# A grouped-query entry with two weight splits moved, and a last norm whose gain ScalarE multiplies ahead of time

## The chip, the cores and the metric

The kernel runs on one core of one Trainium2 chip. The metric is the time of one execution on the device, in microseconds (us). Five engines work side by side, each through its own instructions in order: TensorE (PE, matrix products), VectorE (DVE, element by element), ScalarE (ACT, functions of one tensor), GpSimd (POOL) and SyncE (SP, which here only issues transfers). Transfers between the chip's main memory and the on-chip buffers run on sixteen DMA engines; SP, ACT and POOL each have a queue from which they issue them.

## What is computed

One step of a small backbone with two layers, for 512 latent tokens and 128 prompt tokens with 1024 features each. Layer 0 mixes tokens by latent attention and neighbourhood attention, layer 1 by grouped-query attention (8 query heads, 2 key/value heads of 128 features, with 128 cached positions). Each mixer is followed by a gated feed-forward block, and the whole ends with a root-mean-square norm. Two pieces of the reference matter here: the entry of layer 1 and the last norm.

```
def odd_project(h, w_in, q_norm, k_norm):
    p = h @ w_in
    q, k, v = jnp.split(p, [...], axis=-1)
    q = rms_norm(q.reshape(b, L, GQA_HEADS, GQA_HEAD_DIM), q_norm)
    k = rms_norm(k.reshape(b, L, GQA_KV_HEADS, GQA_HEAD_DIM), k_norm)
    ...

def rms_norm(x, g):
    y = xf * lax.rsqrt(jnp.mean(xf * xf, axis=-1, keepdims=True) + RMS_EPS)
    return (y * g).astype(x.dtype)

y_prompt = rms_norm(xp, norm_final)
y_sample = rms_norm(xs, norm_final)
```

## The kernel before

**Layout.** Features lie on the 128 partitions and tokens along the free dimension. The 1024 features are eight tiles, `x[0]` to `x[7]`, of 128 x 640 (512 latent and 128 prompt tokens). A tile is worked on in two halves of 320 tokens (`HALF`, index c = 0 or 1).

**Split products.** Every float32 product is made from three products of rounded parts. An operand is split into a high part (a rounded copy, written by ACT) and a low part (the difference, written by DVE). `unit` (line 175) loads one 128 x 1024 weight tile and splits it: one ACT instruction (line 184), one DVE instruction (line 185). Its argument `behind` takes one instruction, or a pair (one for ACT, one for DVE), behind which the two are to be issued on their engines. The split weights share three places (tag "w", `bufs=3`), and the raw weights three others (tag "raw").

**What sets the order.** The program is written in one order, but a planner orders each engine's instructions: it goes through the program with estimated costs and puts an instruction that it thinks ready ahead of an earlier one that it thinks is not. Memory is handed out in the same pass. Three things bind it: data dependencies, `after(inst, fn)`, which makes what `fn` issues follow `inst` on the engine of `inst`, and `run`/`sequence`, which do the same for the pieces of PE's work, so that PE follows the order written out by hand (`GQA_FIRST`, line 2028, for head 0).

**The grouped-query entry (lines 1800 to 2040).** PE makes in turns the first half of the keys of group 0 (`keys(0, 0, ...)`, weights `wgk0`), the first half of head 0's queries (`wgq0`), and the values. The values of the 640 new tokens are five products of 128 tokens x 256 (`gvalues`); `gvo[0]` to `gvo[4]` share three banks of PSUM, the accumulator memory, two by two. Each runs over eight feature tiles: the first four use the weights `wgv0`, the last four `wgv1` (line 2011). A sixth value tile comes from the cache (`gcvf`). A loop (line 2015) splits the six into `gvh` and `gvl`; index 4 is the cached tile and index 5 is `gvo[4]`. It keeps the last pair of instructions in the list `valued`. Then head 0's last query products are made, the PSUM banks of keys and values are given back, and new ones are opened for the scores (line 2021, `open_y(s=2)`), so the first scores can't be written before all readers of the value banks are through.

Keys are normalised and rotated on DVE (`knorm`, `rope`), as queries are (`gqr`, `gqh`, `gql`). `weigh` (line 1954) turns a block's scores into exponentials: DVE multiplies the negative maximum by the query's factor `rq`, ACT makes the exponential. Head 0's sequence holds the keys of group 1 (`k0` to `k7`, weights `wgk1`, split at line 1884) and, at its end, head 1's queries (`q0` to `q7`, weights `wgq1`, line 1899).

**The end (lines 1640 to 1730 and 2068 to 2075).** The second half of the last feed-forward product is made in four passes p over pairs of output tiles, each with seven products (`S2, A11, S3, A12, A22, S1, S4`). For p = 3 the tiles are n = 6 and n + 1 = 7. `evac` adds a product to `x` (`residual`, line 319) and adds the square of the result to the norm's sum (`Norm.add`: ACT squares, DVE adds). `nrm.rstd(c)` sums over partitions with one PE product and makes the factor `nrm.rs` by a logarithm and an exponential on ACT. `final` (line 2068) then multiplies each half tile by the gain column and the factor in one DVE instruction (line 2073) and stores it (line 2074), even tiles from ACT's queue and odd ones from SP's. The tile `x[0]` is called `lead` in the profile and the others `xr`. Tile 0 of the first half is scaled before the last residual, tiles 1 to 7 after the last square is added, and then the second half follows.

Of the kernel before, what the change touches and what calls it, by code (L numbers as in the profile page):

```python
# [50 lines left out]
def body(ctx, tc, xT, vecs, crow, wm0, wm0g, wm1, wA, wNV, wNA, wMK, wMV, wOA, wGQ, wGK, wGV, wOC,  # L51
# [267 lines left out]
    def residual(xo, xi, ps, ml, g, n, i):  # L319

        o = HALF[i][0]
        for c0, c1, c in HCOND[i]:
            V.scalar_tensor_tensor(xo[:, c0:c1], ps[:, c0 - o:c1 - o], ml[:, g + n, c:c + 1], xi[:, c0:c1],
                                   ALU.mult, ALU.add)

# [859 lines left out]
    def ffn_open(l):  # L1185
# [13 lines left out]
        return ph, fk, dr, hd, fs, fp, w, pre  # L1199

    def ffn(l, x, pend, hm, nxt, side, opened):
        ph, fk, dr, hd, fs, fp, w0, _ = opened
# [431 lines left out]
        if paired:  # L1634
# [54 lines left out]
            for p in range(4):  # L1689
# [3 lines left out]
                for k, (c, which, to) in enumerate(PLAN):  # L1693
                    j = p * len(PLAN) + k
                    weights(j + LEAD)
                    seventh(j, b[to], which, c in ("S2", "A11", "S1", "S4"))
                    ps = b[to][:, :HT]
                    if c == "S2":
                        S.activation(o["p6"], ps, AF.Copy)
# [7 lines left out]
                    elif c == "A22":  # L1707
                        V.tensor_tensor(o["p1"], ps, o["p1"], ALU.add)
                        evac(n + 1, 0, o["p1"])
                        if p == 3:  # L1710
                            nrm.rstd(0)
                    elif c == "S1":
                        V.tensor_tensor(o["u3"], ps, o["u3"], ALU.add)
                        V.tensor_tensor(o["p6"], ps, o["p6"], ALU.add)
                        if p == 3:
                            residual(x[n], x[n], o["p6"], mods[l], G2, n, 1)
                            evac(n + 1, 1, o["u3"])
                            ended = after(nrm.last, lambda: nxt(x, nrm, 0, range(0, 1)))
                        else:
                            evac(n + 1, 1, o["u3"])  # L1720
                    elif p == 3:
                        after(ended, lambda: evac(n, 1, b["d"]))
                        after(nrm.last, lambda: nxt(x, nrm, 0, range(1, KT)))
                    else:
                        V.tensor_tensor(o["x"], ps, o["p6"], ALU.add)
                        evac(n, 1, o["x"])
# [151 lines left out]
    def keys(v, c, ks):  # L1878
# [4 lines left out]
        if v not in wk:  # L1883
            wk[v] = unit(wGK[v], 1024, f"wgk{v}")
        for k in ks:
# [9 lines left out]

    gqs, rope0, valued = {}, [], []

    def gqa_q(h):
        get = lazy(lambda: unit(wGQ[h], 1024, f"wgq{h}", behind=valued[0] if h == 1 else None))
        qh = gp.tile([P, T], F32R, tag="gqh", bufs=2, name=f"gqh{h}")  # L1900
# [31 lines left out]
    def gqa_scores(h, pts):  # L1932
# [3 lines left out]
        def piece(j):  # L1936
# [17 lines left out]
            def weigh():  # L1954
                V.tensor_tensor(nb, nm, rq[:, j:j + 1], ALU.mult)  # L1955
                S.activation(dst, src, AF.Exp, bias=nb, scale=rq[:, j:j + 1], accum_out=ll[:, j:j + 1])  # L1956
                softmax_tail(pt, ll[:, j:j + 1], f"gr{h}_{j}", n)
                pts.append(pt)
# [50 lines left out]
    for v in range(2):  # L2009
        ksplit(v, 512, 640, ckf[:, P * v:P * v + P])  # L2010
    gvalues(range(5), range(4, KT))
    gvh = [gp.tile([P, 256], F32R, name=f"gvh{i}") for i in range(6)]
    gvl = [gp.tile([P, 256], F32R, name=f"gvl{i}") for i in range(6)]
    srcs = gvo[:4] + [cvf, gvo[4]]
    for i in (0, 1, 2, 3, 5, 4):
        valued[:] = [(S.activation(gvh[i], srcs[i], AF.Copy), V.tensor_tensor(gvl[i], srcs[i], f(gvh[i]), ALU.subtract))]
# [51 lines left out]
    def final(x, nrm, c, ks):  # L2068
        c0, c1 = HALF[c]
        if 0 in ks and c == 1:  # L2070
            nrm.rstd(c)
        for k in ks:
            last = V.scalar_tensor_tensor(x[k][:, c0:c1], x[k][:, c0:c1], vcol(V_NFIN + k), nrm.rs[:, c0:c1], ALU.mult, ALU.mult)
            (nc.sync if k % 2 else nc.scalar).dma_start(yT[:, k, c0:c1], x[k][:, c0:c1])
        return last
# [160 lines left out]
```

## Time and profile before

| What | Value |
|---|---|
| Median of 3 runs | 1488.22 us (1488.15 to 1488.6) |
| Profiled execution, its own time | 1486.84 us |
| Its span | 1485.1 us |
| Granted TensorE clock, mean | 0.997 |
| PE busy | 1440.8 us, 97% of the span |
| DVE busy | 1210.7 us, 82% |
| ACT busy | 763.1 us, 51% |
| Moved by DMA | 228.61 MB, 154 GB/s on average |

The profile is one execution, recorded instruction by instruction. Its times count from the start of the span. A row of a timeline has the start, the duration, the engine, the line, the operation, the tiles (out<-in, with their sizes) and how many were merged; the brackets at its end tell how long the engine sat idle before it and which instruction released it. PEld is PE's loading of weights, which overlaps the products. SPq and ACTq are issues of transfers, not the transfers. A row of windows has, for one stretch, the busy time of PE, PEld, DVE, ACT and POOL, then the granted clock, the busy share of the sixteen DMA engines and the rate in GB/s.

### The profile page before, as it was taken

How to read it: one execution, taken by the hardware profiler on the slowest of the kernel's cores; microseconds unless marked ns; L12 is line 12 of the kernel's file. 1: busy time of each engine (PE TensorE's matmuls, PEld its weight loads, DVE VectorE, ACT ScalarE, POOL GpSimd, SP SyncE). 2: the span in 40 equal slices, each digit the busy share in tenths (PEclk: the TensorE clock that was granted, in tenths of full speed). 3: DMA queues.
4: the chain of work that ended last, by engine and by line, in shares of the span. 5: the costliest groups of instructions: out<-in, count | busy, mean ns of one | idle time of the engine just before them, and what ended most of it. 6: DMA issues, size and time to landing. Idle time of an engine off the chain costs nothing.

```text
span 1485.1 us, 25709 instructions
## 1 busy us (share of the span) xinstructions
PE 1440.8 (97%) x9785; PEld 1390.6 (94%) x9785; DVE 1210.7 (82%) x2278; ACT 763.1 (51%) x1509; POOL 209.9 (14%) x298
## 2 busy tenths in 40 slices
PE   5999989999999999999999999999999999999996
PEld 3988878889999999999999999989999999999996
DVE  5786798975999999977998878775899999954496
ACT  5445687863755444441123666663755555532242
POOL 0325544432000000000002322222000000000000
PEclk9999999999999999999999999999999999999998
DMA  9644511016055555569763301004055556668522
GB/s 370 220 146 141 177 49 33 29 33 209 29 195 176 191 186 183 172 226 340 266 214 125 105 29 45 29 32 133 31 188 175 188 189 208 214 222 304 195 86 72
DMA packets 79900, 228.61 MB, mean 154 GB/s; under 512 B 8864, under 2 KB 14272, under 8 KB 79392
## 3 DMA queue, kind: packets, MB, share of 16 engines
q1 hardware_dynamic: 76544, 219.40, 43.2%
q0 software_dynamic: 1600, 5.14, 0.9%
q10 hardware_dynamic: 1632, 2.43, 0.5%
q8 instruction: 77, 1.26, 0.3%
q14 instruction: 47, 0.39, 0.1%
HBM read 192.23 MB, written 34.69 MB: 153 GB/s over the span
## 4 chain that ended last, share of the span: by engine, by line
PE 84%; DVE 8%; ACT 5%; issue 2%; DMA 1%; SPq 0%; DVEq 0%; POOL 0%; ACTq 0%
PE fg L63 21%; PE fd L63 9%; PE fo L63 8%; PE fu L63 6%; PE gq L63 3%; PE nk L63 2%; PE fo_2b L63 1%; PE fo_0b L63 1%; PE gs L63 1%; PE nq L63 1%; PE fo_2a L63 1%; PE fo_0a L63 1%; PE go L63 1%; PE mod L63 1%; PE fo_4b L63 1%
## 5 line engine op out<-in xcount | busy, mean ns | idle before, releaser
L1774 DVE SCALAR_TENSOR_TENSOR junk<-wm,cb 128x1024 bf16<-128x1024 f32 x62 | 75.7, 1221 | 4.7 <-DMA wm<-in_wm 4.2
L1226 ACT ACTIVATE sg<-g 128x320 f32<-128x320 f32 x34 | 16.0, 472 | 114.8 <-DVE g L1226 114.8
L63 PE MATMUL gq<-h10h,wgq 128*128 128x320 f32 x256 | 66.7, 318 | 0.0
L255 POOL TENSOR_SCALAR h10h<-h10t,gs,mods 128x320 fp32r<-128x320 f32 x4 | 3.5, 887 | 429.5 <-DVE h10t L249 427.8
L1226 DVE SCALAR_TENSOR_TENSOR junk<-wm,cb 128x1024 bf16<-128x1024 f32 x50 | 61.0, 1221 | 0.8
L1226 DVE TENSOR_TENSOR wY<-s,wY 128x1024 fp32r<-128x1024 f32 x40 | 48.8, 1220 | 1.1 <-ACT wY L1226 1.1
L1226 DVE TENSOR_TENSOR wZ<-s,wZ 128x1024 fp32r<-128x1024 f32 x40 | 48.8, 1220 | 0.0
L63 PEld LDWEIGHTS gq<-h10h,wgq 128*128 128x128 f32 x256 | 45.0, 189 | 0.9 <-PE gtp L67 0.2
L1226 ACT ACTIVATE wZ<-s 128x1024 fp32r<-128x1024 f32 x40 | 42.4, 1060 | 0.2
L1226 ACT ACTIVATE wY<-s 128x1024 fp32r<-128x1024 f32 x40 | 42.0, 1049 | 0.0
L1956 ACT ACTIVATE gp<-gs,gb,rq 128x640 f32<-128x640 f32 (+1 forms) x40 | 31.8, 796 | 16.5 <-DVE gb L1955 16.2
L63 PE MATMUL gq<-h10l,wgq 128*128 128x320 f32 x128 | 39.5, 309 | 0.0
L63 PE MATMUL fg<-h11E,wW 128*128 128x320 f32 x240 | 38.7, 310 | 0.0
L63 PE MATMUL fg<-h01q,wX 128*128 128x320 f32 x240 | 38.6, 309 | 0.0
L63 PE MATMUL fg<-h11q,wX 128*128 128x320 f32 x240 | 38.6, 309 | 0.0
L63 PE MATMUL fg<-h01N,wZ 128*128 128x320 f32 x240 | 38.6, 309 | 0.0
L63 PE MATMUL fg<-h11N,wZ 128*128 128x320 f32 x240 | 38.6, 309 | 0.0
L63 PE MATMUL fu<-h01q,wX 128*128 128x320 f32 x240 | 38.6, 309 | 0.0
L63 PE MATMUL fu<-h11q,wX 128*128 128x320 f32 x240 | 38.6, 309 | 0.0
L63 PE MATMUL fg<-h01E,wW 128*128 128x320 f32 x240 | 38.6, 310 | 0.0
L63 PE MATMUL fd<-h01q,wZ 128*128 128x320 f32 x240 | 38.5, 309 | 0.0
L63 PE MATMUL fd<-h11q,wZ 128*128 128x320 f32 x240 | 38.5, 309 | 0.0
(3224 smaller groups left out, 5244.2 us busy)
## 6 DMA issues: line engine op xcount, KB each, us to landing
wm<-in_wm SPq DMA_DIRECT2D x48, 512.0 KB, 3.9
mraw<-in_wm SPq DMA_DIRECT2D x8, 1024.0 KB, 15.3
mraw<-in_wm SPq DMA_DIRECT2D x16, 512.0 KB, 3.6
hr_T<-sp_T SPq DMA_DIRECT2D x21, 320.0 KB, 5.7
hr_B<-sp_B SPq DMA_DIRECT2D x18, 320.0 KB, 6.4
mrow<-in_wm0g POOLq DMA_DIRECT2D x8, 512.0 KB, 7.4
wm<-in_wm0g SPq DMA_DIRECT2D x8, 512.0 KB, 3.4
x<-in_xT SPq DMA_DIRECT2D x8, 320.0 KB, 5.8
```

Of the source, the lines that this page charges most:

```text
L63: cls.last = nc.tensor.matmul(*a, **k)
L255: G.tensor_scalar(h[:, c0:c1], t, self.gsl[:, k, 0:1], self.ml[:, self.sh + k, 0:1], ALU.mult, ALU.add)
L1226: self.last = after(self.last, lambda: op(*a, **k))
L1774: def step(kind, at, line=lambda op, *a, **k: op(*a, **k)):
L1956: S.activation(dst, src, AF.Exp, bias=nb, scale=rq[:, j:j + 1], accum_out=ll[:, j:j + 1])
```

## The change

Entry: the value products over the last four feature tiles are made bank by bank; the loop of value splits begins with the cached tile, so that the last pair is that of `gvo[4]`; the low part of `wgk1` is issued behind that pair's DVE instruction; the split of `wgq1` is issued behind the first pair that `weigh` has issued (exponential on ACT, factor on DVE).

End: `scale_final` multiplies a half tile in place by the final gain on ACT. Twelve such instructions (tiles 0 to 5, both halves) stand in the program at the last pass's product S3, two (tiles 6 and 7, first half) behind the first half's factor, two (second half) behind those tiles' squares. `final` is then a plain product with the factor on DVE. The first scaled tile is issued behind the residual of tile 7, the last residual behind that, and the additions of the squares of tiles 7 and 6 behind it. The first half's stores go out on SP's queue except tiles 4 and 6, which ACT issues behind the second half's factor; the second half's stores alternate as before.

```
     def residual(xo, xi, ps, ml, g, n, i):
...
         for c0, c1, c in HCOND[i]:
-            V.scalar_tensor_tensor(xo[:, c0:c1], ps[:, c0 - o:c1 - o], ml[:, g + n, c:c + 1], xi[:, c0:c1],
-                                   ALU.mult, ALU.add)
+            last = V.scalar_tensor_tensor(xo[:, c0:c1], ps[:, c0 - o:c1 - o], ml[:, g + n, c:c + 1], xi[:, c0:c1],
+                                          ALU.mult, ALU.add)
+        return last
...
+    def scale_final(x, c, k):
+        c0, c1 = HALF[c]
+        S.activation(x[k][:, c0:c1], x[k][:, c0:c1], AF.Copy, scale=vcol(V_NFIN + k))
...
                     seventh(j, b[to], which, c in ("S2", "A11", "S1", "S4"))
                     ps = b[to][:, :HT]
+                    if p == 3 and c == "S3":
+                        for i in range(2):
+                            for k_ in range(n):
+                                scale_final(x, i, k_)
...
                         if p == 3:
                             nrm.rstd(0)
+                            for k_ in (n, n + 1):
+                                scale_final(x, 0, k_)
...
                         if p == 3:
                             residual(x[n], x[n], o["p6"], mods[l], G2, n, 1)
-                            evac(n + 1, 1, o["u3"])
-                            ended = after(nrm.last, lambda: nxt(x, nrm, 0, range(0, 1)))
+                            ended = residual(x[n + 1], x[n + 1], o["u3"], mods[l], G2, n + 1, 1)
+                            ended = after(ended, lambda: nxt(x, nrm, 0, range(0, 1)))
...
                     elif p == 3:
-                        after(ended, lambda: evac(n, 1, b["d"]))
+                        ended = after(ended, lambda: residual(x[n], x[n], b["d"], mods[l], G2, n, 1))
+                        for k_ in (n + 1, n):
+                            after(ended, lambda: nrm.add(x[k_], 1))
+                            scale_final(x, 1, k_)
                         after(nrm.last, lambda: nxt(x, nrm, 0, range(1, KT)))
...
-            wk[v] = unit(wGK[v], 1024, f"wgk{v}")
+            wk[v] = unit(wGK[v], 1024, f"wgk{v}", behind=(None, valued[0][1]))
...
-    gqs, rope0, valued = {}, [], []
+    gqs, rope0, valued, weighed = {}, [], [], []
...
-        get = lazy(lambda: unit(wGQ[h], 1024, f"wgq{h}", behind=valued[0] if h == 1 else None))
+        get = lazy(lambda: unit(wGQ[h], 1024, f"wgq{h}", behind=weighed[0] if h == 1 else None))
...
-                V.tensor_tensor(nb, nm, rq[:, j:j + 1], ALU.mult)
-                S.activation(dst, src, AF.Exp, bias=nb, scale=rq[:, j:j + 1], accum_out=ll[:, j:j + 1])
+                v = V.tensor_tensor(nb, nm, rq[:, j:j + 1], ALU.mult)
+                weighed.append((S.activation(dst, src, AF.Exp, bias=nb, scale=rq[:, j:j + 1], accum_out=ll[:, j:j + 1]), v))
...
-    gvalues(range(5), range(4, KT))
+    for ts in ((0, 1), (2, 3), (4,)):
+        gvalues(ts, range(4, KT))
...
-    for i in (0, 1, 2, 3, 5, 4):
+    for i in (4, 0, 1, 2, 3, 5):
         valued[:] = [(S.activation(gvh[i], srcs[i], AF.Copy), V.tensor_tensor(gvl[i], srcs[i], f(gvh[i]), ALU.subtract))]
...
         if 0 in ks and c == 1:
             nrm.rstd(c)
+            for k in (4, 6):
+                nc.scalar.dma_start(yT[:, k, :HT], x[k][:, :HT])
         for k in ks:
-            last = V.scalar_tensor_tensor(x[k][:, c0:c1], x[k][:, c0:c1], vcol(V_NFIN + k), nrm.rs[:, c0:c1], ALU.mult, ALU.mult)
-            (nc.sync if k % 2 else nc.scalar).dma_start(yT[:, k, c0:c1], x[k][:, c0:c1])
+            last = V.tensor_tensor(x[k][:, c0:c1], x[k][:, c0:c1], nrm.rs[:, c0:c1], ALU.mult)
+            if c or k not in (4, 6):
+                (nc.scalar if c and k % 2 == 0 else nc.sync).dma_start(yT[:, k, c0:c1], x[k][:, c0:c1])
         return last
```

## The prediction

> **What bounds the kernel now.** I read the page first, then TensorE's list of waits over the whole span.
>
> ```profile
> span 1485.1 us, 25709 instructions
> PE 1440.8 (97%) x9785; PEld 1390.6 (94%) x9785; DVE 1210.7 (82%) x2278; ACT 763.1 (51%) x1509; POOL 209.9 (14%) x298
> PE 84%; DVE 8%; ACT 5%; issue 2%; DMA 1%; SPq 0%; DVEq 0%; POOL 0%; ACTq 0%
> PE fn1p L63 <- DVE fn1acc L215: 2.6, 1, 2.6
> PE gs L63 <- DVE gvl L2016: 2.2, 1, 2.2
> ```
>
> PE is busy for 97% and makes 84% of the chain that ended last. Work taken off another engine is therefore worth something in two kinds of place only: where PE stands still, and behind PE's last product. The change touches one of each. The 2.2 us wait is the first score product `gs` of the grouped-query layer, held by the low part of a value tile, `gvl`. The `fn1p` wait belongs to the tail.
>
> **The entry.** The timeline of each engine around that wait (start, duration, engine, line, tiles, and in brackets idle time and releaser):
>
> ```profile
> 817.66 0.40 ACT L2016 ACTIVATE gvh<-gcvf 128x256 fp32r<-128x256 f32 x1
> 842.35 0.27 ACT L1927 ACTIVATE rq<-gr,eps 128x2 f32<-128x2 f32 x1
> 842.49 1.07 ACT L184 ACTIVATE wgq<-wgq1r 128x1024 fp32r<-128x1024 f32 x1
> 843.44 0.40 ACT L2016 ACTIVATE gvh<-gvp 128x256 fp32r<-128x256 f32 x1
> 844.15 0.47 ACT L1909 ACTIVATE gqc<-gq 128x320 f32<-128x320 f32 x1
> 837.32 1.22 DVE L185 TENSOR_TENSOR wgk<-wgk1r,wgk 128x1024 fp32r<-128x1024 f32 x1
> 838.46 0.49 DVE L1916 TENSOR_TENSOR gql<-gqr,gqh 128x320 fp32r<-128x320 f32 x1
> 841.96 1.08 DVE L2016 TENSOR_TENSOR gvl<-gvp,gvh 128x256 fp32r<-128x256 f32 x3
> 843.60 1.23 DVE L185 TENSOR_TENSOR wgq<-wgq1r,wgq 128x1024 fp32r<-128x1024 f32 x1 [0.56 <-ACT wgq L184]
> 844.74 0.42 DVE L2016 TENSOR_TENSOR gvl<-gvp,gvh 128x256 fp32r<-128x256 f32 x1
> 845.08 0.54 DVE L1826 SCALAR_TENSOR_TENSOR gqr<-gqc,vec,tg 128x320 f32<-128x320 f32 x1
> 840.37 0.40 PE L63 MATMUL gvp<-wgv,h10h 128*128 128x256 f32 x2
> 842.78 0.31 PE L63 MATMUL gq<-h10h,wgq 128*128 128x320 f32 x1
> 845.31 0.53 PE L63 MATMUL gs<-gkh,gqh 128*128 128x320 f32 x2 [2.21 <-DVE gvl L2016]
> 846.26 0.31 PE L63 MATMUL gk1a<-h10h,wgk 128*128 128x320 f32 x1
> ```
>
> PE has nothing to do from 842.78 + 0.31 = 843.09 until 845.31. The scores' banks are those of the values, so `gs` waits for the last `gvl`, which ends at 844.74 + 0.42 = 845.16. That one is late because both engines give a weight split the place ahead of it: `wgq1` on ACT from 842.49 to 843.44 (0.95) and on DVE from 843.60 to 844.74 (1.14). Line 1899 means to prevent this, but the list it reads ends with tile 4, which comes from the cache (`gcvf`) and was split at 817.66, so nothing is held back.
>
> The edits. (1) The loop now ends with tile 5, the last value product, and `wgk1`'s low part (DVE only) is pinned behind it. (2) `wgq1` is pinned behind the first exponential of head 0 on ACT and its factor on DVE. (3) The value products run by banks, (0,1), (2,3), (4); the same 60 products, so PE pays nothing, and four of the five splits can start earlier.
>
> Where DVE then stands: before, everything it did from gql's start (838.46) to the end of three gvl's (841.96 + 1.08 = 843.04) is 4.58. Without `wgk1` it starts at 837.32 plus the wait for ACT, say 837.46, and reaches the same point at 842.04; the last gvl adds 0.42: 842.46. Its product ends at 840.37 + 0.40 = 840.77 and its high part is 0.40, so neither is later. PE needs it at 843.09: 0.6 to spare, and the gap of 2.21 closes. I count 2.2.
>
> What is late next. `wgk1`'s low part follows at 842.46 and takes 1.14: 843.60. Its first reader, `gk1a`, comes behind the first scores, 846.26 − 845.31 = 0.95 after 843.09. Spare: 0.4. `wgq1` (0.95 on ACT, 1.14 on DVE) now lies behind the first exponential; what queues behind it on DVE is the next maximum and the query's low part:
>
> ```profile
> 848.41 0.87 ACT L1956 ACTIVATE gp<-gs,gb,rq 128x640 f32<-128x640 f32 x1
> 849.12 0.48 DVE L1916 TENSOR_TENSOR gql<-gqr,gqh 128x320 fp32r<-128x320 f32 x1
> 851.34 0.46 PE L63 MATMUL gs<-gkh,gqh 128*128 128x320 f32 x2
> 856.90 0.36 PE L63 MATMUL gq<-h10h,wgq 128*128 128x320 f32 x1
> ```
>
> The third scores (851.34, then 849.13) need that gql, which ends 5.45 after `gqc` starts at 844.15. `gqc` itself waited behind `wgq1` and gvh; freed, it starts about 843.2, as soon as PE has its product, and gql ends near 848.65: 0.5 to spare. Head 1's query products, which read `wgq1`, move from 856.90 to 854.7; an exponential that ends near 848 leaves over 6 us for a split of 2.1. So I count no loss, but 0 to 0.5 in the range. From there PE runs almost without gaps, so what is won stays won. The lower bound of the entry is the case that another 2.1 us split takes the place (a rival): 0.8.
>
> **The end.** Rows of the three engines behind the last product, then of the stores:
>
> ```profile
> 1469.81 2.80 PE L63 MATMUL fo_3d<-hr_B,wo_3S 128*128 128x320 f32 x18
> 1470.01 0.49 DVE L1713 TENSOR_TENSOR fo_3u<-fo_3c,fo_3u 128x320 f32<-128x320 f32 x1 [1.33 <-PE fo_3c L63]
> 1470.42 0.48 DVE L1714 TENSOR_TENSOR fo_3p<-fo_3c,fo_3p 128x320 f32<-128x320 f32 x1
> 1471.74 0.34 DVE L323 SCALAR_TENSOR_TENSOR xr<-fo_3u,mods,xr 128x128 f32<-128x128 f32 x1
> 1472.62 0.49 DVE L215 TENSOR_TENSOR fn1acc<-fn1acc,fn1sq 128x320 f32<-128x320 f32 x1 [0.54 <-ACT fn1sq L214]
> 1473.03 0.55 DVE L2073 SCALAR_TENSOR_TENSOR lead<-lead,vec,fn1rs 128x320 f32<-128x320 f32 x1
> 1473.49 0.67 DVE L323 SCALAR_TENSOR_TENSOR xr<-fo_3d,mods,xr 128x192 f32<-128x192 f32 x2
> 1474.19 0.47 ACT L214 ACTIVATE fn1sq<-xr 128x320 f32<-128x320 f32 x1 [1.61 <-DVE xr L323]
> 1475.11 3.32 DVE L2073 SCALAR_TENSOR_TENSOR xr<-xr,vec,fn1rs 128x320 f32<-128x320 f32 x7
> 1476.22 0.53 ACT L222 ACTIVATE fn1rs<-fn1p,eps 128x320 f32<-128x320 f32 x1 [1.56 <-PE fn1p L63]
> 1478.81 3.32 DVE L2073 SCALAR_TENSOR_TENSOR xr<-xr,vec,fn1rs 128x320 f32<-128x320 f32 x7
> 1475.68 6.80 SPq L2074 DMA_DIRECT2D out_yT<-xr  x8
> DMA to landing us min/median/max: 1.8/1.9/1.9
> 1460.00:1470.00 10.00, 9.99 (x67) 9.57 (x66) 4.03 (x7) 2.21 (x4) 0.00 (x0) 1.00 0.01 2
> 1478.00:1480.00 2.00, 0.00 (x0) 0.00 (x0) 2.00 (x5) 0.00 (x0) 0.00 (x0) 0.50 1.00 356
> 1474.60:1474.80 0.20, 0.00 (x0) 0.00 (x0) 0.10 (x1) 0.06 (x1) 0.00 (x0) 1.00 1.03 371
> ```
>
> (4) The residual of the last product could start at 1469.81 + 2.80 = 1472.61, but starts at 1473.49, since an addition and the first scaled tile (`lead`) were put ahead of it. In the changed order the first scaled tile starts when the residual before it is done (1471.74 + 0.34) and is over by 1472.6, and the addition comes behind. The residual starts at 1472.66: 0.83 earlier. Square, addition, norm and the first of the seven tiles follow in the old distances, so that tile starts at 1475.11 − 0.83 = 1474.28.
>
> (5) ScalarE multiplies sixteen half tiles by the final gain beforehand, so DVE's last operation becomes a plain product. Price on ACT: 0.47 each by the square, 7.5 in all. Twelve are ready before these 10 us, in which ACT works 2.21 and idles 7.8; that idle time hides them. Without it a square could wait for one of them, 0.47, which is the lower bound's part. The other four lie between the squares and the 1476.22 logarithm, ahead of which ACT idles 1.56. Saving on DVE: fifteen tiles now follow each other at (3.32 − 0.54)/6 = 0.463; a plain tensor product at 1470.42 − 1470.01 = 0.41. That makes 15 × 0.05 = 0.8 if DVE is what the end waits for.
>
> (6) It won't be, I think. A half tile is 128 × 320 × 4 = 164 kB. While DVE delivers one each 0.463 the sixteen DMA engines are at share 1.00 and 356 GB/s. One store alone (1474.60 to 1474.80) has the same full share at 371, so 0.44 to 0.46 per tile is what the engines need, not a queue's doing: each landing takes 1.8 to 1.9, no backlog. At 0.41 per tile a backlog forms, and fifteen tiles take 15 × 0.455 = 6.8 instead of 6.95. The spread over queues issues the same sixteen stores (SP 10, ACT 6); I count nothing for it. The end gains 0.83 + 0.06 (a shorter first tile) + 0.15 = 1.05; bounds 0.4 and 0.83 + 0.06 + 0.85 = 1.74.
>
> **Sum.** 2.2 + 1.05 = 3.25. The profiled execution took 1486.84, of which 1.74 lies around the span; it would take 1483.6. It stands 1.38 below the median of the runs, 1488.22, so the median becomes 1485.0.
>
> **Rivals.** (A) Another split takes the place. Weight tiles rotate through three places; head 2's `wgq2` is loaded by then and not pinned. If it gets the place that `wgq1` no longer claims, it goes ahead of the last gvl: DVE reaches that at 842.46 + 1.14, PE starts near 843.8, then waits for `wgk1` another 0.2 to 0.7. The entry gives 0.8 to 1.3, the end 1.05: 1486.1. For it: ACT put even the logarithm (842.35) ahead of the last gvh. Against: it stands far later in the program than everything of head 0.
>
> (B) The stores keep up with DVE, and the end gives 1.74: 1484.3. For it, only that 371 isn't measured as a ceiling. The Trainium skill would say so too: its page "DMA: Bandwidth & Descriptors", section "Where 436 GB/s comes from", puts the ceiling of the sixteen ports at 435 GB/s, by which a tile would need an estimated 0.38 us; the same section names about 358 GB/s for HBM, and the trace's 356 at full share agrees with that one.
>
> (C) The wait comes back later: exponentials and maxima, about 1.0 earlier (`gqc`, 844.15 to 843.2) while PE is 2.2 earlier, hold the third or fourth scores by 0.5 to 1.5. Sum 1.75 to 2.75: 1486.0.
>
> (D) Slower. If `wgq2` and then `wgq3` take both places freed before the first exponential, `wgq1` gets one only when the keys' weights are done, at 856.90 − 2.2 = 854.7, just when its products are due. PE then waits for 0.95 + 1.23 of split, plus 0.9 of an exponential on ACT and up to 1.2 of another split on DVE: 3.1 to 4.3, against the 3.25 won. From a wait of 3.25 on the kernel is slower; at the middle, 3.7, it takes 1488.7. Against it: `wgq3` must load after `wgk1`'s split has freed its buffer, so it is hardly there in time.
>
> (E) The pins don't bite, since the planner orders the rest anew: only the end's 1.05, 1487.2.
>
> **Numbers.** Forecast 50%, A 13, B 11, C 10, D 8, E 5, and 3 for an order that costs more and that I don't see. A measurement of this kernel can tell about 0.2%, 2.98 us, from no change: faster means below 1485.24. Of the forecast's cases (own range 1484.3 to 1486.0: the entry's loss of up to 0.5, the end's bounds) 35 of the 50 lie below it, and all of B: faster 0.46. Fifteen of the forecast, A, C, E and 5 of D are within: 0.48. Slower has 3 of D, where head 2's split is late in the same way and the wait comes twice (7.4 against 3.25), and the last 3: 0.06. The range reaches from B over A and C to E: 1484.1 to 1487.3.
>
> **What would show it.** No idle time ahead of the first gs; the last gvl ahead of `wgk1` and any `wgq`; gql ahead of the third scores. At the end: fo_3d's residual within 0.1 of PE's last product, tensor products 0.41 apart, landings growing beyond 1.9, DMA share 1.00 until the last store. Wrong if gs still waits, if a wait over 0.5 appears before head 1's queries, or if landings stay at 1.9 with tiles 0.41 apart.

## The result and the profile after

| Kernel | Median (range), executions | Ratio to before, 95% interval |
|---|---|---|
| before | 1488.38 us (1485.84 to 1491.0), 11 | 1 |
| changed | 1484.9 us (1483.39 to 1486.0), 11 | 0.9976 [0.9968, 0.9985] |

The kernel became 3.5 us faster; by the interval 2.2 to 4.8. Its profiled execution took 1484.9 us with a span of 1483.1.

The page of the changed kernel, the totals that were shown of before:

```profile
span 1483.1 us, 25717 instructions
PE 1441.1 (97%) x9785; PEld 1390.4 (94%) x9785; DVE 1209.4 (82%) x2278; ACT 771.3 (52%) x1525; POOL 210.0 (14%) x298
```

PE does the same 9785 products. ACT has sixteen instructions more and works 8.2 us longer (763.1 to 771.3); DVE works 1.3 less. TensorE's list of waits:

```profile
PE fn1p L63 <- DVE fn1acc L215: 1.8, 1, 1.8
...
PE gs L63 <- ACT gvf L2033: 0.4, 1, 0.4
```

The wait at the entry went from 2.2 to 0.4 and has another releaser: no longer the low part of a value, but `gvf`, ACT's copy of the last value tile for the cache output.

The two spans differ by 1.94. To put that in its places I cut each trace at three points that a timeline gives: the first product of the grouped-query keys (`gk0a`), the first score product (`gs`), and the end of PE's last product (`fo_3d`).

| us | before | changed | difference |
|---|---|---|---|
| start to first `gk0a` | 812.42 | 813.21 | +0.79 |
| first `gk0a` to first `gs` | 32.89 | 31.03 | −1.86 |
| first `gs` to the end of `fo_3d` | 627.31 | 627.37 | +0.06 |
| end of `fo_3d` to the end of the span | 12.45 | 11.52 | −0.93 |

So the entry gives 1.86, the end 0.93, and nothing of the entry's gain is given back on the 627 us between. The 0.79 ahead of the entry belongs to the execution: the engines' orders up to there are the same in both kernels, and over all traces of this study that point lies between 811.0 and 813.2.

The entry of the changed kernel, the timeline (start, duration, engine, line, tiles, idle time before and its releaser):

```profile
838.17 0.37 ACT L2031 ACTIVATE gvh<-gvp 128x256 fp32r<-128x256 f32 x1
840.87 0.39 ACT L2031 ACTIVATE gvh<-gvp 128x256 fp32r<-128x256 f32 x1 [2.33 <-DVE gvl L2031]
842.59 0.66 ACT L2031 ACTIVATE gvh<-gvp 128x256 fp32r<-128x256 f32 x2 [0.49 <-DVE gvl L2031]
843.80 0.38 ACT L2033 ACTIVATE gvf<-gvp 128x256 f32<-128x256 f32 x1
849.15 1.05 ACT L184 ACTIVATE wgq<-wgq1r 128x1024 fp32r<-128x1024 f32 x1
851.47 1.06 ACT L184 ACTIVATE wgq<-wgq2r 128x1024 fp32r<-128x1024 f32 x1
839.83 0.55 DVE L1842 SCALAR_TENSOR_TENSOR kro01b<-kn,ones,tg 64x320 f32<-64x320 f32 x1
840.41 0.42 DVE L2031 TENSOR_TENSOR gvl<-gvp,gvh 128x256 fp32r<-128x256 f32 x1
843.01 0.76 DVE L2031 TENSOR_TENSOR gvl<-gvp,gvh 128x256 fp32r<-128x256 f32 x2 [0.45 <-ACT gvh L2031]
843.68 1.22 DVE L185 TENSOR_TENSOR wgk<-wgk1r,wgk 128x1024 fp32r<-128x1024 f32 x1
844.24 0.56 PE L63 MATMUL gs<-gkh,gqh 128*128 128x320 f32 x2 [0.35 <-ACT gvf L2033]
```

The order is the one that the change asks for: the last `gvl` (its end is 843.01 + 0.76 = 843.77) ahead of `wgk1` (843.68) and far ahead of `wgq1` (849.15), and `wgq2` behind that. But the values' reads take turns. ACT's second `gvh` waits 2.33 until DVE's first `gvl` ends, and the kernel puts these two tiles into one bank of PSUM; that `gvl`, whose `gvh` was ready at 838.54, stands on DVE behind the rotation of the keys (`kro01b`, 839.83). At the end of the chain of turns `gvf` reads the bank of the last tile once more, behind its `gvl`, and `gs` starts when `gvf` is done.

The end of the changed kernel, the timeline, and in a fence of its own the row of its stores:

```profile
1469.83 1.78 PE L63 MATMUL fo_3d<-hr_B,wo_3S 128*128 128x320 f32 x11
1470.99 0.49 DVE L2090 TENSOR_TENSOR lead<-lead,fn1rs 128x320 f32<-128x320 f32 x1
1471.62 0.56 ACT L1204 ACTIVATE xr<-xr,vec 128x320 f32<-128x320 f32 x1
1471.64 0.68 DVE L323 SCALAR_TENSOR_TENSOR xr<-fo_3d,mods,xr 128x192 f32<-128x192 f32 x2 [0.17 <-PE fo_3d L63]
1473.27 2.90 DVE L2090 TENSOR_TENSOR xr<-xr,fn1rs 128x320 f32<-128x320 f32 x7
1474.81 0.47 ACT L223 ACTIVATE fn1rs<-fn1rs 128x320 f32<-128x320 f32 x1
1476.08 0.49 DVE L2090 TENSOR_TENSOR lead<-lead,fn1rs 128x320 f32<-128x320 f32 x1
1476.48 2.90 DVE L2090 TENSOR_TENSOR xr<-xr,fn1rs 128x320 f32<-128x320 f32 x7
```

```profile
DMA to landing us min/median/max: 1.8/2.3/2.8
```

The residual starts 0.03 behind PE's last product (1469.83 + 1.78 = 1471.61), where it had started 0.88 behind. DVE's tiles follow each other at (2.90 − 0.49)/6 = 0.40, and the landings grow from 1.8 to 2.8: the stores no longer keep up.

### The profile page after: what moved, and what is told of

It is laid out like the page before. It is cut to its first block, busy times and chain, and to the rows that moved or that the text cites. A ratio compares the mean times of both kernels' runs of the same rounds, so it can differ in the third digit from the quotient of the medians.

```text
span 1483.1 us, 25717 instructions
## 1 busy us (share of the span) xinstructions
PE 1441.1 (97%) x9785; PEld 1390.4 (94%) x9785; DVE 1209.4 (82%) x2278; ACT 771.3 (52%) x1525; POOL 210.0 (14%) x298
## 4 chain that ended last, share of the span: by engine, by line
PE 83%; DVE 7%; ACT 5%; DMA 3%; issue 2%; ACTq 0%; DVEq 0%; POOL 0%; SPq 0%
PE fg L63 21%; PE fd L63 9%; PE fo L63 8%; PE fu L63 6%; PE gq L63 3%; DMA mraw<-in_wm 3%; PE nk L63 2%; PE fo_2b L63 1%; PE fo_0b L63 1%; PE gs L63 1%; PE fo_2a L63 1%; PE fo_0a L63 1%; PE go L63 1%; PE nq L63 1%; PE fo_4b L63 1%
```

## The experiments

Eleven other kernels ran, and the kernel before once more. "Gap" is PE's idle time ahead of the first `gs`; the other columns are the stretches of above. Each row is one profiled execution.

| Kernel | gap | `gk0a` to `gs` | `gs` to end of `fo_3d` | end of `fo_3d` to end of span | span |
|---|---|---|---|---|---|
| before | 2.21 | 32.89 | 627.31 | 12.45 | 1485.06 |
| changed | 0.35 | 31.03 | 627.37 | 11.52 | 1483.12 |
| the entry's edits alone | 0.34 | 31.03 | 627.34 | 12.38 | 1483.00 |
| the end's edits alone | 2.21 | 32.90 | 627.29 | 11.53 | 1484.97 |
| final gain on DVE | 0.33 | 31.00 | 627.33 | 11.58 | 1482.40 |
| without the first half's stores | 0.35 | 31.02 | 627.34 | 11.05 | 1482.08 |
| keys' weights unpinned | 0.56 | 31.24 | 627.33 | 11.52 | 1482.75 |
| values not bank by bank | 0.07 | 30.75 | 627.35 | 11.53 | 1482.43 |
| `wgq1` behind the values | 0.77 | 31.44 | 628.27 | 11.52 | 1482.26 |
| last value read once from PSUM | 0 | 30.52 | 627.81 | 11.52 | 1481.93 |
| old order at the end | 0.36 | 31.04 | 627.34 | 12.30 | 1483.54 |
| stores on the old queues | 0.36 | 31.04 | 627.38 | 11.49 | 1481.80 |
| two more tiles ahead, values not bank by bank | 0.05 | 30.74 | 627.30 | 11.18 | 1482.11 |
| before, again | 2.20 | 32.89 | 627.30 | 14.64 | 1486.14 |

Where nothing changes, a column repeats within 0.1 (but for the last row); what differs by more in the span is the time ahead of `gk0a`.

**The two parts, each alone.** The entry's edits on the kernel before:

```diff
-    gvalues(range(5), range(4, KT))
+    for ts in ((0, 1), (2, 3), (4,)):
+        gvalues(ts, range(4, KT))
-    for i in (0, 1, 2, 3, 5, 4):
+    for i in (4, 0, 1, 2, 3, 5):
...
+ (the pins of wgk1 and wgq1 and the list `weighed`, as in the change)
```

> Only the entry's edits, the end as before. Theory (the two places are independent and add up): idle time of PE ahead of the first scores as in the changed kernel, 0.35 us instead of 2.21, so 1.86 us less in the span, and from the last product's end to the span's end 12.45 us as before. Ratio near 1 - 1.86/1488 = 0.9987. Rival (the entry's gain is given back later, rival C): the first scores come 1.86 earlier, but the distance from them to PE's last product, 627.3 us in both kernels, grows.

And the end's edits on the kernel before, the entry left as it was:

> Only the end's edits, the entry as before. Theory: idle time ahead of the first scores 2.21 us as before, and from PE's last product to the span's end 11.45 us as in the changed kernel instead of 12.45: 1.0 less. Ratio near 0.9993. Rival: part of the end's 1.0 belongs to the entry (a shift of the planner's order), then the tail is longer than 11.45.

Measured: 1484.72 us against 1488.27 (ratio 0.9974 [0.9965, 0.9983]), and 1487.0 (0.9988 [0.9978, 0.9997]). In the traces each part gives, alone, what it gives in the changed kernel: the entry 1.86, the end 0.92, and neither touches the other's place. The times show more than the traces: 3.55 and about 1.3. For the end, 0.92 lies inside the interval (0.4 to 3.3); for the entry, 1.86 lies outside (2.5 to 5.2). The last experiment goes after that.

**What sets the end.** The gain back on DVE, the new order kept:

```diff
-            last = V.tensor_tensor(x[k][:, c0:c1], x[k][:, c0:c1], nrm.rs[:, c0:c1], ALU.mult)
+            last = V.scalar_tensor_tensor(x[k][:, c0:c1], x[k][:, c0:c1], vcol(V_NFIN + k), nrm.rs[:, c0:c1], ALU.mult, ALU.mult)
... (and no scale_final)
```

> The changed kernel with the final gain back on VectorE: no ScalarE multiplications, the last operation with two factors at 0.463 us per tile instead of 0.40; the new order of the last residual and the stores' queues are kept. Theory (the DMA engines set the end): the tail stays within 0.2 us of 11.45, since fifteen tiles need 15 x 0.455 = 6.8 us of transfer anyway; landings fall back to about 1.9. Rival B (DVE sets the end): the tail grows by 15 x 0.06 = 0.9 to 12.35.

Measured: 1484.17 us in one execution, the end 11.58. Rows of that kernel, the timeline and the landings:

```profile
1472.49 3.32 DVE L2083 SCALAR_TENSOR_TENSOR xr<-xr,vec,fn1rs 128x320 f32<-128x320 f32 x7
1476.19 3.32 DVE L2083 SCALAR_TENSOR_TENSOR xr<-xr,vec,fn1rs 128x320 f32<-128x320 f32 x7
```

```profile
DMA to landing us min/median/max: 1.8/1.9/1.9
```

DVE is at 0.463 a tile again, the landings show no backlog, and the end is 0.06 longer. So the sixteen scalings by ScalarE bring 0.06; the stores set the pace. Two windows, the first of the changed kernel, the second of this one (columns as before; the last two are the DMA engines' busy share and GB/s):

```profile
1477.00:1479.00 2.00, 0.00 (x0) 0.00 (x0) 2.00 (x6) 0.00 (x0) 0.00 (x0) 0.50 0.99 355
```

```profile
1477.00:1479.00 2.00, 0.00 (x0) 0.00 (x0) 2.00 (x6) 0.00 (x0) 0.00 (x0) 0.50 0.99 357
```

The same full share and the same rate, whether DVE delivers a tile each 0.40 or each 0.463.

**The first half's stores left out** (the eight stores of the first half aren't made, so half of the output is missing; all arithmetic stays):

```diff
-            for k in (4, 6):
-                nc.scalar.dma_start(yT[:, k, :HT], x[k][:, :HT])
...
-            if c or k not in (4, 6):
+            if c:
```

> The changed kernel without the eight stores of the first half (the first 320 tokens of the output are not written). Theory (a backlog of transfers sets the end): without them the second half's stores find the DMA engines free, landings fall from up to 2.8 to about 1.9 us, and the tail shrinks by the backlog of 0.9 us to about 10.55; what is left is DVE's own pace. Rival (DVE sets the end): the tail stays at 11.45.

Measured: 1484.14 us in one execution, the end 11.05, that is 0.47 shorter, where 0.9 was expected. The landings of this kernel:

```profile
DMA to landing us min/median/max: 1.8/2.1/2.2
```

The size was wrong, not the direction: the second half alone builds up a backlog of its own. Eight tiles at 0.455 − 0.40 are 0.44, and the landings do grow by 0.4. What the first half's stores cost is only their own part, about as much again.

**The pin of the keys' weights** taken off (`wgk1`'s low part free, as before; the rest as changed):

```diff
-            wk[v] = unit(wGK[v], 1024, f"wgk{v}", behind=(None, valued[0][1]))
+            wk[v] = unit(wGK[v], 1024, f"wgk{v}")
```

> The changed kernel, but the low part of the second key weights (1.14 us on DVE) is not pinned behind the last value tile. Theory (that split was one of two that kept DVE from the values): it moves back ahead of the queries' low part, and the idle time ahead of the first scores grows from 0.35 to about 1.5 us. Rival: the pin of the first head's query weights alone is what counts, idle time stays below 0.6.

Measured: 1484.85 us in one execution, the gap 0.56 where 1.5 was expected. The timeline:

```profile
837.57 1.22 DVE L185 TENSOR_TENSOR wgk<-wgk1r,wgk 128x1024 fp32r<-128x1024 f32 x1
840.81 0.42 DVE L2031 TENSOR_TENSOR gvl<-gvp,gvh 128x256 fp32r<-128x256 f32 x1
843.46 0.38 ACT L2033 ACTIVATE gvf<-gvp 128x256 f32<-128x256 f32 x1 [0.21 <-DVE gvl L2031]
843.90 0.56 PE L63 MATMUL gs<-gkh,gqh 128*128 128x320 f32 x2 [0.56 <-ACT gvf L2033]
```

`wgk1` is back where it stood in the kernel before, ahead of all values (837.57). This execution comes to the entry 0.55 earlier than that of the changed kernel, whose first `gvl` would so start at 840.41 − 0.55 = 839.86; here it starts 0.95 later, and yet `gvf` only 0.21 later (843.46 against 843.80 − 0.55). Most of the delay is made up on the way, since DVE does the later `gvl` in pairs. Of the 1.14 that the prediction took off DVE's load here, 0.2 reaches PE. What the rival says of the wait, below 0.6, is what came.

**The order of the value products** put back:

```diff
-    for ts in ((0, 1), (2, 3), (4,)):
-        gvalues(ts, range(4, KT))
+    gvalues(range(5), range(4, KT))
```

> The changed kernel with the value products in the old order (all five tiles for each feature tile), so that all value banks are ready only at the end. Theory (the banks' readers work one after the other, ACT and DVE in turn, so an early bank helps): idle time ahead of the first scores grows from 0.35 to between 0.7 and 1.2 us. Rival (DVE's amount of work sets it): it stays at 0.35.

Measured: 1484.2 us in one execution, and the opposite of what was expected: the gap is smaller, 0.07. The timeline:

```profile
841.00 0.64 ACT L2030 ACTIVATE gvh<-gvp 128x256 fp32r<-128x256 f32 x2
842.55 0.40 ACT L2030 ACTIVATE gvh<-gvp 128x256 fp32r<-128x256 f32 x1
843.07 0.38 ACT L2032 ACTIVATE gvf<-gvp 128x256 f32<-128x256 f32 x1
841.41 2.00 DVE L2030 TENSOR_TENSOR gvl<-gvp,gvh 128x256 fp32r<-128x256 f32 x5
```

With all tiles ready at about the same time, DVE does the five `gvl` in one run, to 843.41. That is no earlier than in the changed kernel (843.77, less 0.40 by which this execution runs ahead), so the early splits that the bank order allows gain nothing. But `gvf` starts at 843.07, while the last `gvl` still runs: that one lies in another bank. The first `gs` (843.55) starts 0.15 behind the end of the last `gvl`, as in the kernel before (845.16 to 845.31), and 0.10 behind the end of `gvf`, where it is 0.05 in the changed kernel; so it waits for the `gvl`, not for a copy behind it. The bank order put the tile that is read three times at the end of the chain, which costs 0.29. (That the banks differ is read from the overlap; the rows leave the tiles' numbers out.)

**`wgq1` pinned behind the values** instead of the first exponential:

```diff
-        get = lazy(lambda: unit(wGQ[h], 1024, f"wgq{h}", behind=weighed[0] if h == 1 else None))
+        get = lazy(lambda: unit(wGQ[h], 1024, f"wgq{h}", behind=valued[0] if h == 1 else None))
```

> The changed kernel with the first head's query-weight split pinned behind the last value tile only, not behind the first exponential. Theory: the idle time ahead of the first scores stays at 0.35 or, if the split gets ahead of the copy gvf on ACT (0.95 us), grows to about 1.3; the rest of the layer is unchanged. Rival: the pin behind the exponential is needed for the first scores as such, idle time about 1.5 or more.

Measured: 1484.75 us in one execution; the gap 0.77, and 0.90 more is lost later. Its timeline:

```profile
841.08 1.07 ACT L184 ACTIVATE wgq<-wgq1r 128x1024 fp32r<-128x1024 f32 x1
842.02 0.39 ACT L2033 ACTIVATE gvf<-gvp 128x256 f32<-128x256 f32 x1
842.79 1.09 ACT L184 ACTIVATE wgq<-wgq2r 128x1024 fp32r<-128x1024 f32 x1
842.47 0.56 PE L63 MATMUL gs<-gkh,gqh 128*128 128x320 f32 x2 [0.77 <-ACT gvf L2033]
984.64 0.33 PE L63 MATMUL gs<-gkh,gqh 128*128 128x128 f32 x1 [0.43 <-ACT gp L1970]
```

The value tiles now have their places, and the split goes ahead of `gvf`, the reader that the pin doesn't name; `wgq2` follows at once. Of the 0.90, about 0.3 shows at the third scores and 0.6 around 984.6, where a score waits for an exponential; that the rest of the layer would stay as it is was expected wrongly. So the pin behind the exponential, in place of the one behind the values, is worth 0.41 + 0.90 = 1.3, more than the wait itself shows.

**The last value tile read once from PSUM** (`gvf` copied first; its high and low part made from the copy):

```diff
-    srcs = gvo[:4] + [cvf, gvo[4]]
... (the loop of value splits, moved behind the copy)
     gvf = tmp("gvf")
     S.activation(gvf[:, :256], gvo[4], AF.Copy)
...
+    srcs = gvo[:4] + [cvf, gvf[:, :256]]
... (the loop)
```

> The changed kernel, but the last value bank has one reader: ACT copies it once to gvf, and the split of that tile is made from gvf. Theory (what is left of the wait, 0.35 us, is the turn of ACT, DVE, ACT on that bank, ended by the copy gvf): the idle time goes to 0 to 0.1, the span falls by 0.3. Rival (DVE's low parts of the other banks end as late): 0.2 to 0.35 stay.

Measured: 1484.77 us in one execution. The gap is gone, `gs` comes 0.51 earlier (the gap of 0.35, and 0.16 by which it now overlaps the product ahead of it), and 0.44 of it is given back, most of it at the next step:

```profile
842.62 0.42 DVE L2034 TENSOR_TENSOR gvl<-gvf,gvh 128x256 fp32r<-128x256 f32 x1 [0.31 <-ACT gvh L2034]
842.96 1.22 DVE L185 TENSOR_TENSOR wgk<-wgk1r,wgk 128x1024 fp32r<-128x1024 f32 x1
844.23 0.57 PE L63 MATMUL gk1a<-h10h,wgk 128*128 128x320 f32 x2 [0.31 <-DVE wgk L185]
```

With the scores no longer late, the pinned `wgk1` is: PE waits for it at `gk1a`. But this edit also makes `wgk1` later. The low part of the last tile now waits for a copy and for a high part made from it, so that `wgk1` starts 0.41 later behind `gk0a` (842.96 − 812.08 = 30.88) than in the changed kernel (843.68 − 813.21 = 30.47). With the values not bank by bank, where `gs` comes 0.29 earlier and `wgk1` isn't held up, nothing is lost behind `gs` (627.35). So closing the gap in this way brings 0.07, where 0.3 was expected.

**The order at the end, and the queues.** The old order around the last product, scaling and queues as changed:

```diff
-                            ended = residual(x[n + 1], x[n + 1], o["u3"], mods[l], G2, n + 1, 1)
-                            ended = after(ended, lambda: nxt(x, nrm, 0, range(0, 1)))
+                            evac(n + 1, 1, o["u3"])
+                            scale_final(x, 1, n + 1)
+                            ended = after(nrm.last, lambda: nxt(x, nrm, 0, range(0, 1)))
...
-                        ended = after(ended, lambda: residual(x[n], x[n], b["d"], mods[l], G2, n, 1))
-                        for k_ in (n + 1, n):
-                            after(ended, lambda: nrm.add(x[k_], 1))
-                            scale_final(x, 1, k_)
+                        after(ended, lambda: evac(n, 1, b["d"]))
+                        scale_final(x, 1, n)
```

> The changed kernel with the old order around PE's last product: the addition of the norm and the first scaled tile stand ahead of the last residual on DVE again; ScalarE's scaling ahead of time and the spread of the stores stay. Theory (the order alone made the end's gain): the residual starts about 0.8 later behind PE's last product, 0.17 becomes 0.9 to 1.0, and the end goes from 11.52 back to 12.2 to 12.4. Rival (the DMA engines' backlog sets the end whatever the order, or the plain product and the scaling made the gain): the end stays within 0.2 of 11.52.

Measured: 1485.31 us in one execution, the end 12.30, 0.78 longer. Its timeline:

```profile
1469.76 1.48 PE L63 MATMUL fo_3d<-hr_B,wo_3S 128*128 128x320 f32 x9
1471.65 0.49 DVE L2089 TENSOR_TENSOR lead<-lead,fn1rs 128x320 f32<-128x320 f32 x1
1472.06 0.67 DVE L323 SCALAR_TENSOR_TENSOR xr<-fo_3d,mods,xr 128x192 f32<-128x192 f32 x2
```

PE ends at 1471.24, the residual starts 0.82 later, behind the first scaled tile. So the order makes 0.78 of the end's gain of 0.93.

The stores on the queues of the kernel before:

```diff
-            for k in (4, 6):
-                nc.scalar.dma_start(yT[:, k, :HT], x[k][:, :HT])
...
-            if c or k not in (4, 6):
-                (nc.scalar if c and k % 2 == 0 else nc.sync).dma_start(yT[:, k, c0:c1], x[k][:, c0:c1])
+            (nc.sync if k % 2 else nc.scalar).dma_start(yT[:, k, c0:c1], x[k][:, c0:c1])
```

> The changed kernel with the stores on the queues of the kernel before (odd tiles from SP's, even ones from ScalarE's, each right behind its product). Theory (the spread is worth nothing, since the sixteen DMA engines carry both queues and are full): the end 11.4 to 11.6, the landings 1.8 to 2.8 as in the changed kernel. Rival (the spread keeps the first half's stores out of ScalarE's way, whose logarithm and exponential of the last norm come in the same microseconds): the end 0.2 to 0.5 longer.

Measured: 1483.86 us in one execution, the end 11.49, 0.03 shorter. The spread over the queues is worth nothing.

**Two more tiles of the first half ahead of the last residual, and the values not bank by bank**: the version that the runs point to.

```diff
-                            ended = after(ended, lambda: nxt(x, nrm, 0, range(0, 1)))
+                            ended = after(ended, lambda: nxt(x, nrm, 0, range(0, 3)))
...
-                        after(nrm.last, lambda: nxt(x, nrm, 0, range(1, KT)))
+                        after(nrm.last, lambda: nxt(x, nrm, 0, range(3, KT)))
...
-    for ts in ((0, 1), (2, 3), (4,)):
-        gvalues(ts, range(4, KT))
+    gvalues(range(5), range(4, KT))
```

> The changed kernel with two edits: the value products run for all five tiles row by row of the weights again, which left a wait of 0.07 before the first score where the changed kernel has 0.36; and the first three final products of the first half, not the first alone, stand ahead of the last residual on DVE, so their stores leave before the second half's do. Theory (what sets the end is the sixteen DMA engines, and work that is moved ahead of PE's last product is taken off it): the wait before the first score 0.0 to 0.1; from the end of PE's last product to the end of the span two stores fewer of 0.455 remain, 11.52 becomes about 10.7; median 1.1 below the changed kernel's 1484.7 to 1484.9, about 1483.7. Rival (the two tiles on DVE, 0.8 in all, hold up the last residual and with it square, norm and every later tile): the end gets no shorter, 11.5 to 12.3, and the median is 1484.4 or above.

Measured: 1484.04 us, ratio 0.9968 [0.9955, 0.9981] to before; one of the six executions took 5004.63 us and is left out of the ratio. In the trace the entry is 0.29 and the end 0.34 shorter than in the changed kernel; against the changed kernel's 0.9976 the times can't tell the two apart. The end gave 0.34 where 0.8 was expected, and the timeline shows why:

```profile
1469.74 1.19 PE L63 MATMUL fo_3d<-hr_B,wo_3S 128*128 128x320 f32 x7
1470.71 0.89 DVE L2089 TENSOR_TENSOR xr<-xr,fn1rs 128x320 f32<-128x320 f32 x2
1471.52 0.68 DVE L323 SCALAR_TENSOR_TENSOR xr<-fo_3d,mods,xr 128x192 f32<-128x192 f32 x2
1474.68 0.47 ACT L223 ACTIVATE fn1rs<-fn1rs 128x320 f32<-128x320 f32 x1
1475.18 0.49 DVE L2089 TENSOR_TENSOR lead<-lead,fn1rs 128x320 f32<-128x320 f32 x1
```

The two tiles hold the residual until 0.59 behind PE's last product (1470.93), and the second half's first tile (1475.18) now starts right behind the norm's factor (1474.68 + 0.47), which that residual made late. In the changed kernel the factor was ready at 1475.28 and waited 0.8 for DVE. Theory and rival both hold in part.

**The kernel before, once more**, with nothing edited.

> The kernel before once more, with nothing edited, for a second profiled execution and more times of it. What is asked: executions of the kernel before and of the kernel with the end's edits alone lie 1482.8 to 1490.4 in span, those with the entry's edits mostly 1481.5 to 1483.6, and the medians of the entry's edits alone differ by 3.5 to 3.9 where the two traces show 1.86. Theory (the wait at the entry isn't 2.2 in every execution: where the splits come in another order of time it is longer, up to 2 to 4 more, and the changed order takes that away too): in an execution longer than the profiled 1485.06 the excess lies between the first product of the grouped-query keys and the end of PE's last product, that is 32.89 to the first score or 627.31 behind it grow by it. Rival (the excess lies ahead of the grouped-query layer, in layer 0, and has nothing to do with the change): the first product of the keys starts later than 812.4 by the excess, and 32.89 and 627.31 stay within 0.2. The time against the kernel before: ratio 1.000.

Measured: 1488.74 us, ratio 1.0002 [0.9994, 1.0011]; the profiled execution took 1487.91, 1.07 more than the first. Neither theory nor rival holds: the entry repeats to the hundredth (32.89, 627.30), `gk0a` is 1.11 earlier, and the end is 14.64, 2.19 longer. The stores of this execution, and the window of its DMA queues from 1474 to 1481:

```profile
L2074 SPq DMA_DIRECT2D out_yT<-xr x8: 332/338/1545, 1474.6 to 1481.7; - x8
L2074 ACTq DMA_DIRECT2D out_yT<-xr x6: 338/344/2005, 1475.6 to 1481.8; - x6
DMA to landing us min/median/max: 1.8/3.3/4.9
```

```profile
GB/s 0 0 0 0 0 0 0 0 307 358 264 7 0 205 351 423 315 344 337 373 337 337 336 242 7 7 7 7 15 22 80 358 329 388 373 337 359 358 351 359
...
q8 instruction: 1, 0.02, 1.7%
```

An issue of these stores takes 332 to 350 ns in the first execution; here one on SP took 1545 and one on ACT 2005 ns, side by side, and for about 1.2 us next to nothing moved (seven slices of 0.175 us at 7 to 80 GB/s), though DVE delivered its tiles at the same distances behind PE's end as ever. In that window lies one packet of a queue that carries instructions, not data: 16 kB from 1476.64 to 1478.50; both late issues end at 1478.9. In the other thirteen traces that packet came 2.9 us ahead of PE's end, or behind the last store, or not in the last 20 us; in none between the stores. That it stopped the issues is a coincidence in time seen once, not shown. So one execution of the kernel before lost 2 us at its end, and this is one place from which scatter can come.

## Why the prediction was right, and where not

The time was forecast at 1485.0 and is 1484.9. From the trace's own time the forecast was 1483.6 and it came to 1484.9, of which 0.79 lies ahead of the entry; the steps gave 2.79 where 3.25 was counted. The median moved by 3.5, more than the traces show; that forecast and median agree within 0.1 is luck, and better than the steps behind them. Of its own signs of being wrong one came, `gs` still waits (0.35); the others didn't: no wait over 0.5 stands between `gs` and head 1's queries, and the landings grew. What the signs asked of the end (the residual within 0.1 of PE's last product, tiles about 0.41 apart, full share) came too, with 0.03, 0.40 and 0.99.

**The entry, 2.2 forecast, 1.86 measured.** The cause was right: with the splits held back the wait went, and with one of them let in again ahead of `gvf` it came back (0.77, and 0.90 later). Three parts of the step failed. "The loop now ends with tile 5", and it was read as the late one of before. It can't have been: in the kernel before, `gvf`, which reads that tile's bank behind its `gvl`, started at 843.71, ahead of the late `gvl` (844.74). By the loop's order the late one was tile 3, whose bank is shared; the rows leave the numbers out, so that is inferred. "Four of the five splits can start earlier" is the part that has the wrong sign: it costs 0.29. And the last reader of the banks isn't a `gvl` but `gvf`, which the prediction doesn't name; it ends 0.30 after PE ran dry (843.88). What the step left out is that ACT and DVE take turns on a bank. The Trainium skill says why a program must let them: its page "PSUM — Partial Sum Buffer", section "PSUM bank collisions raise a hardware error", has it that two engines on one bank and the same partitions at once collide, reads among them. The trace agrees in that ACT's `gvh` waits 2.33 for DVE's `gvl` of the same bank; no run here tried the collision.

The row of `gvf` in the kernel before:

```profile
843.71 0.41 ACT L2018 ACTIVATE gvf<-gvp 128x256 f32<-128x256 f32 x1
```

DVE was to reach the end of the last `gvl` at 842.46; it did at 843.77, which less the 0.79 of this execution is 842.98. So the 0.6 of air became 0.1, and `gvf` used it up.

**The pins.** Of the 1.14 for `wgk1`, 0.2 counts; that it would not be late itself, "spare: 0.4", was right: PE doesn't wait for it, not even with `gs` 0.29 earlier (values not bank by bank). It waits 0.31 with `gs` 0.51 earlier and `wgk1` 0.41 later. `wgq1` behind the first exponential in place of the last value is worth 1.3, the most of the edits at the entry that were tried alone.

**Nothing given back:** right, 627.37 against 627.31. Rivals A and C fall by that number and by the order (`wgq2` at 851.47 behind `wgq1` at 849.15), D with them: the third head's weights never came first. E falls, since the pins hold.

**The end, 1.05 forecast, 0.93 measured.** The residual, "0.83 earlier", came 0.85 earlier, and 0.78 of the end's gain goes when the old order is put back. The rest of 0.21 (the first tile 0.06, the stores 0.15) measured 0.1: the seven tiles start 0.83 earlier behind PE's end and the last store lands 0.93 earlier. That the stores, not DVE, set the end was right: 0.06 is lost with DVE back at 0.463. Rival B falls with that; of the two figures that it weighed, the one of about 358 GB/s (the Trainium skill, "DMA: Bandwidth & Descriptors", "Where 436 GB/s comes from") is the one that the 355 and 357 of the two windows agree with. The landings grow to 2.8, as the backlog asked.

**ScalarE's price** was set at 0.47 by the square; it is 0.56. The Trainium skill has the difference: by its page "ScalarE: Activation LUTs", section "What ACT_TABLE_LOAD costs", an ACTIVATE takes 186 ns and 0.833 ns for each element, and a scale or bias read from a column adds about 93 ns, which gives an estimate of 0.45 for the square and 0.55 for the scaling. The trace agrees with 0.47 and 0.56. It stays hidden: sixteen are 9.0 in all, and with the gain on DVE instead the end isn't shorter (11.58).

**What stays open.** Why the timed executions differ more than the traces at the entry (3.55 against 1.86). The second trace of the kernel before excludes a wait at the entry that is longer in that execution, and shows one loss at the end, 2.19. Whether such losses come more often without the entry's edits, two executions can't tell. One thing goes with the excess: the granted clock on record for each timed execution. Among those of the entry's edits alone and of the kernel before beside it, the executions at 0.997, the clock of both traces, have mean spans of 1482.53 (three) and 1484.65 (four): 2.12 apart, near the 2.06 by which the traces' spans differ. The kernel before has ten of its nineteen at 0.993 or 0.994, with a mean of 1487.67; of the ten with the entry's edits none lies below 0.995. Whether the clock makes those executions longer, or a longer end, where the clock is at 0.50, lowers its mean, no trace shows: none was taken of an execution below 0.995.

## What to carry to other kernels

Where a product waits for a bank, list every reader of that bank and which engine each is on, the copy for an output too: the last reader sets the start, and here readers on two engines went in turns, so that results which finished earlier weren't read out earlier. Pin work that isn't needed yet behind work that is needed sooner, and look at what the pin makes the next bound. In a tail bound by its stores, what counts is when they start (0.78 here) and how many are left behind the last product (0.34 with two moved ahead); a faster engine in front of full transfer engines brought 0.06 of the 0.8 that its own durations promised.

## What the runs showed of the hardware that was not expected

A store of 128 rows of 1280 bytes takes the sixteen DMA engines 0.46 us (163.84 kB at 355 to 357 GB/s), whether they are fed each 0.40 or each 0.463 us.

An issue of a store of the output, 332 to 353 ns in the first trace of the kernel before and up to 455 ns in those of the other kernels, took 1545 and 2005 ns in one execution, on both queues at once, around a 16 kB transfer of instructions, with 2.19 us lost at the end.

The first product of the grouped-query keys comes between 811.0 and 813.2 us in the fourteen traces, with the same work ahead of it in all, while unchanged stretches behind it repeat within 0.1, but for the one end with the late issues.
